# Chunk inverses four products at a time in the quarters of the array, and scan steps ranked ahead of the fill

## The chip, the core and the metric

The kernel runs on one core of a Trainium2 chip. The metric is device time in microseconds (us) of one execution. The engines are named as the profile names them: PE is TensorE (PEld its weight loads), DVE is VectorE, ACT is ScalarE, POOL is GpSimd, SP issues transfers.

## What is computed

Two blocks run one after the other on a sequence of 256 latent tokens and 256 context tokens, width 1024, all float32. The first has a feed-forward part, a mixer and a second feed-forward part. The second has two layers; its first layer mixes by RWKV-7 heads beside latent attention (MLA), each layer ends in a mixture of experts. Modulation vectors come from matrices `w_ada` and `ada_w`.

The change lies in the RWKV scan of the second block. Eight heads of width 64, two directions, states from the context carried to the latents:

```python
def step(S, inp):
    r_t, w_t, k_t, v_t, a_t, b_t = inp
    sa = jnp.einsum('bhij,bhj->bhi', S, a_t)
    S = (S * w_t[:, :, None, :] + sa[..., None] * b_t[:, :, None, :]
         + v_t[..., None] * k_t[:, :, None, :])
    return S, jnp.einsum('bhij,bhj->bhi', S, r_t)
...
y_c, states_c = rwkv_scans(r_c, v_c, dirs_c, (zero, zero))
y_l, _ = rwkv_scans(r_l, v_l, dirs_l, states_c)
```

## The kernel before

**The scan in chunks.** The kernel does not step through tokens. It cuts 256 tokens into 4 chunks of 64 and needs, for each head, direction and chunk, the inverse of a 64x64 unit triangular matrix. `rwkv` handles one half of the heads (four) at a time; two head pairs x 4 chunks give x = 0 to 7, and each pair holds one head in partitions 0 to 63 and the other in 64 to 127 (`par`). So one tile of 128 x 512 holds sixteen 64x64 matrices. The scan runs for two halves on the context and two on the latents: four inverses.

**The inverse.** A first set of products builds the matrices from `AR` and `BK` (masked by `copy_predicated` into a tile that ScalarE had filled with identities); then six levels double the block that is inverted. A level takes `Gt` times `tm` into PSUM tile `pg` (from `sm()`) and `tm` times `Gt` into `pgt` (from `acc()`); VectorE multiplies both by masks `lv` into new tiles `ab_T` and `ab_Gt`. The last level has the second product alone, copied by ScalarE. The product of each head stays in its own half of the partitions: operands and result in rows 0 to 63, or in rows 64 to 127, that is in the two quadrants on the array's diagonal. The two directions (`d`) alternate. Every float32 product of this kind shows as two records (passes) in the trace, and as one instruction in the orders below. One inverse has 416 products: 32 for each of 6 sets and 16 in the last, for two directions.

**What lies beside it.** `mixer_ab` interleaves generators by a string: `0` and `1` are the two halves of the scan, `L` the latent attention, `O` the output projection, `T` one step of `tick()`, the fill. On the context the fill is the first block's feed-forward part and its modulation; on the latents it is the modulation of the second layer. The framework's scheduler then orders the instructions of each engine by rank (the place in the program) and by its own timeline of what is ready.

**Weights.** `w()` loads 512 KB into one of four buffers `w_raw` over SP's queue; ScalarE rounds it to `w_hi`, VectorE (POOL for some) forms `w_lo`; two buffers each. A product by weights is three matmuls: `h_h,w_hi`, `h_l,w_hi`, `h_h,w_lo` (L238 to L240). The modulation multiplies `w_raw` directly in 128x32 column tiles (`sm<-w_raw,aT`, L224).

**PSUM.** In the two phases concerned `acc()` and `sm()` draw on one pool: three tiles on the context and four on the latents.

Of the kernel before, what the change touches and what calls it, by code (L numbers as in the profile page):

```python
# [14 lines left out]
U32 = mybir.dt.uint32  # L15
AF = mybir.ActivationFunctionType
OP = mybir.AluOpType
# [115 lines left out]
class _Net:  # L133
# [926 lines left out]
    def col(self, n, j):  # L1060
        c = self.pcn[n] + j
        return self.pc[:, c:c + 1]
# [36 lines left out]
    def mixer_ab(self, ht, keep, is_x, result):  # L1099

        nc, io = self.nc, self.io
        w_in = io["ab_w_in_2"][0]
        pool = nc.gpsimd
        col = self.col


        def mixed(blocks, dst):
            def use(pair, ps):
                n = len(pair)
                pp, s = self.t(2, 258, name="ab_pp"), self.t(2, 256, name="ab_s")  # L1110
                pool.memset(pp[:, :, 0:258:257], 0.0)
                self.act(pp[:, :n, 1:257], ps[:, :n, :])
                self.tt(s[:, :n], pp[:, :n, 0:256], pp[:, :n, 2:258], OP.add, e=pool)
                for a, (c0, _) in enumerate(pair):
                    b = c0 // 128
                    o = dst(b)
                    self.act(o, ps[:, a, :], scale=col(("rw_mu_2", -1.0), b))
                    self.stt(o, s[:, a], col(("rw_mu_2", 0.5), b), o, OP.mult, OP.add)
            return self.proj_T(ht, w_in, 8, [(128 * b, 128) for b in blocks], use)
        LO = [self.t(256, name="ab_lo") for _ in range(3)]  # L1120
        for _ in mixed((12, 13, 14), lambda b: LO[b - 12]):
            pass
        self.tick()

        w2, a2 = [self.t(512, name="ab_lw") for _ in range(2)]
        self.dma(w2, io["rw_w2_2"][0].rearrange("d r f -> (d r) f"))
        self.dma(a2, io["rw_a2_2"][0].rearrange("d r f -> (d r) f"))
        self.act(LO[0], LO[0], AF.Tanh)
        self.act(LO[2], LO[2], AF.Sigmoid)
        sg = {}  # L1130
        for d in range(2):
            r = slice(64 * d, 64 * d + 64)
            b0 = self.row("rw_w0_2", d * 512, 512)
            for i in range(2):
                pz = self.acc()
                self.mm(pz, LO[0][r, i * 128:(i + 1) * 128], w2[r, :])
                sg[d, i] = self.t(512, name="ab_sg")
                self.tt(sg[d, i], pz, b0, OP.add)
                self.act(sg[d, i], sg[d, i], AF.Sigmoid)
        outs = {}  # L1140
        r0, r1 = [self.rwkv(hf, mixed, LO, sg, a2, keep, is_x, outs) for hf in range(2)]
        la = self.within(self.stream("la0" if is_x else "lac", s=8, h=2, sm=2), self.mla(ht, keep, is_x, outs))
        w_out = io["ab_w_out_2"][0]

        def leave():

            todo, use = {"la": (4, 512), 0: (2, 0), 1: (2, 256)}, None
            while todo:
                key = next((z for z in todo if z in done), None)
                if key is None:  # L1150
                    yield
                    continue
                nk, r = todo.pop(key)
                use = use or self.gated_to(*result())
                for c in (0, 512):
                    ps = [self.acc() for _ in range(2)]
                    for k0 in range(0, nk, 2):
                        wt = self.w(w_out[r + k0 * 128:r + k0 * 128 + 256, c:c + 512], 2, 512, nc.gpsimd if c else None)
                        for i in range(2):
                            for k in range(2):  # L1160
                                self.mm3(ps[i], outs[key].pair(k0 + k, i * 128, 128), (wt[0][:, k, :], wt[1][:, k, :]),
                                         k0 + k == 0, k0 + k == nk - 1)
                            if k0 + 2 == nk:
                                use(i, c, 512, ps[i])
                        yield
        out = self.within(self.stream("ad0", sm=2) if is_x else self.slots, leave())
        done = set()
        streams = {"0": (r0, 0), "1": (r1, 1), "L": (la, "la"), "O": (out, "O")}
        for z in ORDERS["x" if is_x else "ctx"]:
            if z == "T":  # L1170
                self.tick()
            elif z in streams:
                g, name = streams[z]
                if next(g, self) is self:
                    done.add(name)
        for g, name in (streams[z] for z in "0L1O"):
            if g is out:
                done.update((0, 1, "la"))
            for _ in g:
                self.tick()  # L1180
            done.add(name)

    def rwkv(self, hf, mixed, LO, sg, a2, keep, is_x, outs):

        nc, lv, col = self.nc, self.lv, self.col
# [6 lines left out]
        for d in range(2):  # L1192
            r = slice(64 * d, 64 * d + 64)
            ps = self.sm()
# [15 lines left out]
        ps = self.head_spread(rr)  # L1210
# [7 lines left out]
        AR, BK, Dc = [], [], []  # L1218
        ks = self.t(2, 256, name="ab_ks")
        for d in range(2):  # L1220
            E, En = self.t(2, 4, 65, name="ab_E"), self.t(2, 4, 64, name="ab_En")
            pe = self.sm()
            for b, c in enumerate(blk):
                for i in range(2):
                    o = b * 256 + i * 128
# [32 lines left out]
        self.tt(ks, ks, R, OP.mult, e=pool)  # L1258


        def v8(z):
            return z.rearrange("p (x t) -> p x t", x=8)

        def mk(d, l, kept):
            return lv[:, 12 * kept + 6 * d + l, None, :].to_broadcast([128, 8, 64])
        GG = {}
        for d in range(2):
            tm, Gt = self.t(8, 64, name="ab_T"), self.t(8, 64, name="ab_Gt")
            for which, dst in ((0, tm), (1, Gt)):
                ps = self.sm() if which else self.acc()  # L1270
                for x in range(8):
                    for par in range(2):
                        r = slice(64 * par, 64 * par + 64)
                        a, b = AR[d][r, x // 4, x % 4, 0, :], BK[d][r, x // 4, x % 4, 1 - x % 2, :]
                        if which:
                            a, b = b, a
                        self.mm(ps[r, x * 64:(x + 1) * 64], a, b)
                self.act(dst, self.id64[:, None, :].to_broadcast([128, 8, 64]))
                m = self.lm.bitcast(U32)[:, 2 * which + d, None, :].to_broadcast([128, 8, 64])
                nc.vector.copy_predicated(dst, m, v8(ps))  # L1280
            GG[d] = tm, Gt
            yield
        for l in range(1, 7):
            for d in range(2):
                tm, Gt = GG[d]
                pgt = self.acc()
                pg = self.sm() if l < 6 else None
                halves = (slice(0, 64), slice(64, 128))
                for x in range(8):
                    for r in halves if l < 6 else ():  # L1290
                        self.mm(pg[r, x * 64:(x + 1) * 64], Gt[r, x, :], tm[r, x, :])
                    for r in halves:
                        self.mm(pgt[r, x * 64:(x + 1) * 64], tm[r, x, :], Gt[r, x, :])
                tm, Gt = self.t(8, 64, name="ab_T") if l < 6 else None, self.t(8, 64, name="ab_Gt")
                if l < 6:
                    self.tt(tm, v8(pg), mk(d, l, 0), OP.mult)
                    self.tt(Gt, v8(pgt), mk(d, l, 1), OP.mult)
                else:
                    self.act(Gt, v8(pgt))
                GG[d] = tm, Gt  # L1300
                yield

        VT = self.t(2, 256, name="ab_VT")
        ps = self.sm()
# [41 lines left out]
        for step in range(4):  # L1346
            now, G1 = [ahead.pop((step, d)) for d in range(2)], []
            Zs = [keep.get(("Z", d, hf)) for d in range(2)]
            for d, (c, ru, SC, UV, ST) in enumerate(now):
                Z = Zs[d]  # L1350
                pg = self.sm()
                at = [(pg[r, b * 64:(b + 1) * 64], r.start) for h, r, b in heads]
                parts = [[(*o, SC[:, h, 0:64], UV[:, h, :]) for o, (h, r, b) in zip(at, heads)]]
# [30 lines left out]
            for d, (c, ru, SC, UV, ST) in enumerate(now):  # L1384
                tok = slice(64 * c, 64 * c + 64)
                py = self.sm()
                at = [(py[r, b * 64:(b + 1) * 64], r.start) for h, r, b in heads]
                parts = [[(*o, UV[:, h, :], SC[:, h, 64:128]) for o, (h, r, b) in zip(at, heads)]]
# [15 lines left out]
        ps = self.sm()  # L1404
# [5 lines left out]
        ps = self.sm()  # L1410
# [743 lines left out]
```

## Time and profile before

| | us |
|---|---|
| median of 3 runs | 2460.53 (2452.52 to 2464.1) |
| the profiled execution | 2464.48 |
| its span (first to last instruction) | 2462.6 |
| TensorE busy | 2201.6 |
| VectorE busy | 1462.5 |
| ScalarE busy | 1149.5 |

The four inverses lie at 225 to 386 us and 565 to 699 us (context, first and second half of the heads), and at 1484 to 1560 us and 1621 to 1704 us (latents). A stretch of the trace is described by the busy time of each engine in it, the granted clock of TensorE (1.00 is 2.4 GHz, 0.50 is 1.2 GHz) and what the transfer engines moved.

### The profile page before, as it was taken

What the parts mean: (1) busy time and instruction counts of PE and PEld (TensorE: products, weight loads), DVE (VectorE), ACT (ScalarE), POOL (GpSimd) and SP (SyncE); (2) the same over time, 40 slices, a digit from 0 to 9 for tenths busy, and PEclk for the clock granted to TensorE, in tenths of its full rate; (3) what the DMA queues carried; (4) which work ended last, traced back from release to release, by engine and by line L of the source; (5) the groups of instructions that cost most, each with busy time, mean ns of one, the idle gap of its engine ahead of it and who ended that gap; (6) DMA issues with size and microseconds to landing.
All of it is one profiled execution on the core that took longest, in us unless ns stands there. A gap on an engine that the chain in (4) does not pass through costs nothing. (4 is left out here: it accounts for less than half of the span.)

```text
span 2462.6 us, 42928 instructions
## 1 busy us (share of the span) xinstructions
PE 2201.6 (89%) x17189; PEld 1768.4 (72%) x17189; DVE 1462.5 (59%) x2405; ACT 1149.5 (47%) x1787; POOL 482.1 (20%) x402
## 2 busy tenths in 40 slices
PE   5898999989999889988899889989899987788996
PEld 2686667878888668877799778667676666457774
DVE  2444343576555745887655544554666677756776
ACT  1453223465455434554444453434347754555673
POOL 1232000042000320000100133242215533001442
PEclk9899999999999899999999999979899998898998
DMA  8766777554444433431766556720249983224996
GB/s 289 236 199 214 251 243 257 183 163 126 129 124 135 142 125 103 137 98 40 235 190 185 162 163 203 253 77 19 95 157 342 385 308 123 52 72 142 307 326 239
DMA packets 371881, 445.07 MB, mean 181 GB/s; under 512 B 21224, under 2 KB 274264, under 8 KB 371672
## 3 DMA queue, kind: packets, MB, share of 16 engines
q1 hardware_dynamic: 362744, 409.99, 52.3%
q0 software_dynamic: 4320, 15.47, 2.0%
q10 hardware_dynamic: 4608, 16.78, 1.7%
q8 instruction: 137, 2.24, 0.4%
q14 instruction: 72, 0.59, 0.1%
HBM read 415.99 MB, written 26.96 MB: 180 GB/s over the span
## 5 line engine op out<-in xcount | busy, mean ns | idle before, releaser
L246 ACT ACTIVATE w_hi<-w_raw 128x1024 fp32r<-128x1024 f32 (+2 forms) x550 | 575.3, 1050 | 785.1 <-PE acc L240 298.2
L252 DVE TENSOR_TENSOR w_lo<-w_raw,w_hi 128x1024 fp32r<-128x1024 f32 (+1 forms) x466 | 586.8, 1265 | 460.6 <-ACT w_hi L246 455.1
L238 PE MATMUL acc<-h_h,w_hi 128*128 128x256 f32 (+1 forms) x1392 | 400.3, 288 | 16.4 <-ACT w_hi L246 11.5
L240 PE MATMUL acc<-h_h,w_lo 128*128 128x256 f32 (+1 forms) x1392 | 401.0, 288 | 4.2 <-DVE w_lo L252 3.2
L239 PE MATMUL acc<-h_l,w_hi 128*128 128x256 f32 (+1 forms) x1392 | 392.9, 282 | 1.0 <-DVE h_l L252 0.6
L238 PEld LDWEIGHTS acc<-h_h,w_hi 128*128 128x128 f32 (+1 forms) x1392 | 264.1, 190 | 29.1 <-ACT w_hi L246 15.5
L240 PEld LDWEIGHTS acc<-h_h,w_lo 128*128 128x128 f32 (+1 forms) x1392 | 263.7, 189 | 18.2 <-DVE w_lo L252 6.2
L252 POOL TENSOR_TENSOR w_lo<-w_raw,w_hi 128x1024 fp32r<-128x1024 f32 (+1 forms) x84 | 202.4, 2424 | 345.1 <-ACT w_hi L246 336.4
L239 PEld LDWEIGHTS acc<-h_l,w_hi 128*128 128x128 f32 (+1 forms) x1392 | 264.1, 190 | 2.5 <-DVE h_l L252 1.3
L224 PE MATMUL sm<-w_raw,aT 128*32 128x256 f32 x1344 | 113.9, 413 | 23.8 <-DMA w_raw<-in_w_ada 11.0
L239 PE MATMUL acc<-w_lo,h_h 128*128 128x512 f32 (+1 forms) x304 | 119.0, 392 | 0.8 <-DVE w_lo L252 0.8
L238 PE MATMUL acc<-w_hi,h_h 128*128 128x512 f32 (+1 forms) x304 | 112.7, 396 | 5.4 <-ACT h_h L246 3.8
L240 PE MATMUL acc<-w_hi,h_l 128*128 128x512 f32 (+1 forms) x304 | 116.9, 387 | 0.1
L239 PE MATMUL acc<-w_lo,mo_e_h 128*128 128x512 f32 x256 | 105.3, 411 | 12.1 <-DVE w_lo L252 11.4
L252 POOL TENSOR_TENSOR rs_r<-rs_t,mhalf 128x1 f32<-128x1 f32 (+2 forms) x37 | 39.5, 1069 | 354.1 <-DVE rs_t L256 352.8
L238 PE MATMUL acc<-w_hi,f_a_h 128*128 128x512 f32 x264 | 103.4, 415 | 4.8 <-ACT w_hi L246 2.9
L238 PE MATMUL acc<-w_hi,mo_e_h 128*128 128x512 f32 x256 | 104.0, 406 | 2.9 <-ACT w_hi L246 2.8
L239 PE MATMUL acc<-w_lo,f_a_h 128*128 128x512 f32 x264 | 105.9, 408 | 0.0
L224 PE MATMUL acc<-ab_Gt,ab_T 64*64 64x64 f32 x1536 | 103.7, 228 | 0.0
L240 PE MATMUL acc<-w_hi,f_a_l 128*128 128x512 f32 x264 | 102.5, 401 | 0.0
L240 PE MATMUL acc<-w_hi,mo_e_l 128*128 128x512 f32 x256 | 101.7, 397 | 0.0
L224 PEld LDWEIGHTS acc<-ab_Gt,ab_T 64*64 64x64 f32 x1536 | 82.7, 139 | 25.1 <-issue 21.5
(530 smaller groups left out, 4381.8 us busy)
## 6 DMA issues: line engine op xcount, KB each, us to landing
w_raw<-in_ffn_w_in SPq DMA_DIRECT2D x132, 512.0 KB
w_raw<-in_ada_w SPq DMA_DIRECT2D x96, 512.0 KB
w_raw<-in_w_ada SPq DMA_DIRECT2D x72, 512.0 KB
w_raw<-in_ffn_w_out SPq DMA_DIRECT2D x66, 512.0 KB
w_raw<-in_moe_w_gate SPq DMA_DIRECT2D x128, 256.0 KB
w_raw<-in_moe_w_up SPq DMA_DIRECT2D x128, 256.0 KB
w_raw<-in_moe_w_down SPq DMA_DIRECT2D x64, 512.0 KB
w_raw<-in_mix_w_in SPq DMA_DIRECT2D x42, 512.0 KB
```

Of the source, the lines that this page charges most:

```text
L224: self.nc.tensor.matmul(out, lhsT=lhsT, rhs=rhs, start=start, stop=stop, **kw)
L238: mm(out, lhsT=l[0], rhs=r[0], start=start, stop=False)
L239: mm(out, lhsT=l[0], rhs=r[1], start=False, stop=False)
L240: mm(out, lhsT=l[1], rhs=r[0], start=False, stop=stop)
L246: self.nc.scalar.activation(out, in_, f, **kw)
L252: (e or self.nc.vector).tensor_tensor(out=out, in0=a, in1=b, op=op)
```

## The change

First, each step of the two scan streams runs inside `high_priority(offset=5000)`: its instructions get a rank 5000 places ahead of where they stand, so the scheduler prefers them to fill, attention and output projection whenever they are ready.

Second, in the inverse the eight x are parted by `q = x % 2`. Both factors of one q lie in one tile `ab_T` (2 x 4 x 64), and so do both products in one PSUM tile (`acc()` for q = 0, `sm()` for q = 1). `quarters` issues the products so that four neighbours have the row halves and column halves (0,0), (1,1), (0,1), (1,0): for q = 1 the result lands in the other half of the partitions, and comes back a level later. The last level stays a loop of its own, on the diagonal. The number of products and the number and size of the element-wise instructions stay as they were.

```diff
--- before.py
+++ after.py
@@ -1171,7 +1171,10 @@
                 self.tick()
             elif z in streams:
                 g, name = streams[z]
-                if next(g, self) is self:
+
+                with self.tc.high_priority(offset=5000) if z in "01" else contextlib.nullcontext():
+                    ended = next(g, self) is self
+                if ended:
                     done.add(name)
         for g, name in (streams[z] for z in "0L1O"):
             if g is out:
@@ -1258,47 +1261,62 @@
         self.tt(ks, ks, R, OP.mult, e=pool)
 
 
-        def v8(z):
-            return z.rearrange("p (x t) -> p x t", x=8)
-
-        def mk(d, l, kept):
-            return lv[:, 12 * kept + 6 * d + l, None, :].to_broadcast([128, 8, 64])
+
+
+        def mk(d, l):
+            return lv[:, 6 * d + l:24:12, None, :].to_broadcast([128, 2, 4, 64])
+
+        def quarters(parts, at, l):
+            for j in range(4):
+                for which in range(2):
+                    for q in range(2):
+                        for par in range(2):
+                            r, o = [64 * (par ^ (q & (z % 2))) for z in (l, l + 1)]
+                            self.mm(parts[q][o:o + 64, (which * 4 + j) * 64:(which * 4 + j + 1) * 64], *at(q, j, which, slice(r, r + 64)))
+
+        def v4(z):
+            return z.rearrange("p (w j t) -> p w j t", w=2, j=4)
         GG = {}
         for d in range(2):
-            tm, Gt = self.t(8, 64, name="ab_T"), self.t(8, 64, name="ab_Gt")
-            for which, dst in ((0, tm), (1, Gt)):
-                ps = self.sm() if which else self.acc()
-                for x in range(8):
-                    for par in range(2):
-                        r = slice(64 * par, 64 * par + 64)
-                        a, b = AR[d][r, x // 4, x % 4, 0, :], BK[d][r, x // 4, x % 4, 1 - x % 2, :]
-                        if which:
-                            a, b = b, a
-                        self.mm(ps[r, x * 64:(x + 1) * 64], a, b)
-                self.act(dst, self.id64[:, None, :].to_broadcast([128, 8, 64]))
-                m = self.lm.bitcast(U32)[:, 2 * which + d, None, :].to_broadcast([128, 8, 64])
-                nc.vector.copy_predicated(dst, m, v8(ps))
-            GG[d] = tm, Gt
+            ps = [self.acc(), self.sm()]
+
+            def factors(q, j, which, r):
+                x = 2 * j + q
+                a, b = AR[d][r, x // 4, x % 4, 0, :], BK[d][r, x // 4, x % 4, 1 - q, :]
+                return (b, a) if which else (a, b)
+            quarters(ps, factors, 0)
+            GG[d] = []
+            for q in range(2):
+                dst = self.t(2, 4, 64, name="ab_T")
+                self.act(dst.rearrange("p w j t -> p (w j) t"), self.id64[:, None, :].to_broadcast([128, 8, 64]))
+                m = self.lm.bitcast(U32)[:, d:4:2, None, :].to_broadcast([128, 2, 4, 64])
+                nc.vector.copy_predicated(dst, m, v4(ps[q]))
+                GG[d].append(dst)
             yield
-        for l in range(1, 7):
+        for l in range(1, 6):
             for d in range(2):
-                tm, Gt = GG[d]
-                pgt = self.acc()
-                pg = self.sm() if l < 6 else None
-                halves = (slice(0, 64), slice(64, 128))
-                for x in range(8):
-                    for r in halves if l < 6 else ():
-                        self.mm(pg[r, x * 64:(x + 1) * 64], Gt[r, x, :], tm[r, x, :])
-                    for r in halves:
-                        self.mm(pgt[r, x * 64:(x + 1) * 64], tm[r, x, :], Gt[r, x, :])
-                tm, Gt = self.t(8, 64, name="ab_T") if l < 6 else None, self.t(8, 64, name="ab_Gt")
-                if l < 6:
-                    self.tt(tm, v8(pg), mk(d, l, 0), OP.mult)
-                    self.tt(Gt, v8(pgt), mk(d, l, 1), OP.mult)
-                else:
-                    self.act(Gt, v8(pgt))
-                GG[d] = tm, Gt
+                ps = [self.acc(), self.sm()]
+
+                def factors(q, j, which, r):
+                    tm, Gt = [GG[d][q][r, z, j, :] for z in range(2)]
+                    return (tm, Gt) if which else (Gt, tm)
+                quarters(ps, factors, l)
+                got = []
+                for q in range(2):
+                    got.append(self.t(2, 4, 64, name="ab_T"))
+                    self.tt(got[q], v4(ps[q]), mk(d, l), OP.mult)
+                GG[d] = got
                 yield
+        for d in range(2):
+            ps = self.acc()
+            for x in range(8):
+                for r in (slice(0, 64), slice(64, 128)):
+                    tm, Gt = [GG[d][x % 2][r, z, x // 2, :] for z in range(2)]
+                    self.mm(ps[r, x * 64:(x + 1) * 64], tm, Gt)
+            Gt = self.t(8, 64, name="ab_Gt")
+            self.act(Gt, ps.rearrange("p (x t) -> p x t", x=8))
+            GG[d] = None, Gt
+            yield
 
         VT = self.t(2, 256, name="ab_VT")
         ps = self.sm()
```

**Order on PE, context, first half of the heads.** Before, products of the inverse stand among modulation (`w_raw,aT`) and feed-forward (`f_a`) products:

```order
L224 MATMUL acc<-ab_Gt,ab_T 64x64
L224 MATMUL sm<-w_raw,aT_137 32x256 x4
L224 MATMUL acc<-ab_Gt,ab_T 64x64 x3
L224 MATMUL sm<-ab_T,ab_Gt 64x64 x2
L224 MATMUL acc<-ab_Gt,ab_T 64x64
L224 MATMUL sm<-w_raw,aT_137 32x256
L238 MATMUL acc<-w_hi,f_a_h 128x512 x2
L224 MATMUL sm<-w_raw,aT_137 32x256 x3
L224 MATMUL acc<-ab_Gt,ab_T 64x64
L224 MATMUL sm<-ab_T,ab_Gt 64x64 x2
L224 MATMUL acc<-ab_Gt,ab_T 64x64 x2
```

After, at the same place of the inverse (`ab_T` names both factors; a level of one direction has 32 products):

```order
L224 MATMUL acc<-ab_T 64x64 x15
L224 MATMUL sm<-ab_T 64x64 x14
L224 MATMUL acc<-ab_T 64x64
L224 MATMUL sm<-ab_T 64x64 x2
L224 MATMUL acc<-ab_T 64x64 x15
L224 MATMUL sm<-ab_T 64x64 x14
L224 MATMUL acc<-ab_T 64x64
L224 MATMUL sm<-ab_T 64x64 x2
L224 MATMUL acc<-ab_T 64x64 x15
L224 MATMUL sm<-ab_T 64x64 x14
```

The fill has moved out: from the first to the last product of this inverse there were 71 pieces before, spread over the instructions 1087 to 2259 of PE, and 5 pieces after, in 1085 to 1552. Fill alone now fills the instructions 1930 to 2610, where it uses 72 weight tiles; from 2610 on the two orders agree. A piece of 15 in `acc` followed by 14 in `sm` holds products of one q each.

**Order on PE, latents, first half of the heads.** Before, a level stands unbroken by the fill's products:

```order
L224 MATMUL sm<-ab_T,ab_Gt 64x64 x2
L224 MATMUL acc<-ab_Gt,ab_T 64x64 x2
L224 MATMUL sm<-ab_T,ab_Gt 64x64 x2
L224 MATMUL acc<-ab_Gt,ab_T 64x64 x2
L224 MATMUL sm<-ab_T,ab_Gt 64x64 x2
L224 MATMUL acc<-ab_Gt,ab_T 64x64 x2
L224 MATMUL sm<-ab_T,ab_Gt 64x64 x2
L224 MATMUL acc<-ab_Gt,ab_T 64x64 x2
```

After, a later level has one product by weights (`h`, `w`) between every one or two of its own:

```order
L238 MATMUL acc<-h_h,w_hi 128x256
L224 MATMUL acc<-ab_T 64x64 x2
L239 MATMUL acc<-h_l,w_hi 128x256
L224 MATMUL acc<-ab_T 64x64 x2
L240 MATMUL acc<-h_h,w_lo 128x256
L224 MATMUL sm<-ab_T 64x64
L238 MATMUL acc<-h_h,w_hi 128x256
L224 MATMUL sm<-ab_T 64x64
L239 MATMUL acc<-h_l,w_hi 128x256
L224 MATMUL acc<-ab_T 64x64 x2
L240 MATMUL acc<-h_h,w_lo 128x256
L224 MATMUL acc<-ab_T 64x64 x2
```

The pieces of this inverse go from 17 to 45. Counted over the stretch of the context (instructions 1087 to 5400), PE changes between divisions of the array (128x128, 128x32, 64x64 and so on) 463 times before and 345 after; over that of the latents (8380 to 10500) 275 times before and 322 after.

## Rows read from the trace of the kernel before

**Rows 1.** The page: engine totals, granted clock by slice, two costliest groups

```profile
PE 2201.6 (89%) x17189; PEld 1768.4 (72%) x17189; DVE 1462.5 (59%) x2405; ACT 1149.5 (47%) x1787; POOL 482.1 (20%) x402
...
PEclk9899999999999899999999999979899998898998
...
L246 ACT ACTIVATE w_hi<-w_raw 128x1024 fp32r<-128x1024 f32 (+2 forms) x550 | 575.3, 1050 | 785.1 <-PE acc L240 298.2
...
L252 DVE TENSOR_TENSOR w_lo<-w_raw,w_hi 128x1024 fp32r<-128x1024 f32 (+1 forms) x466 | 586.8, 1265 | 460.6 <-ACT w_hi L246 455.1
```

**Rows 2.** Table of stretches; the first row names the columns

```profile
core 0: us, PE busy (x) PEld busy (x) DVE busy (x) ACT busy (x) POOL busy (x), PEclk, DMA share, GB/s
10.00:80.00 70.00, 48.97 (x380) 25.48 (x380) 13.71 (x41) 13.05 (x22) 5.29 (x8) 0.88 0.89 308
80.00:217.00 137.00, 125.23 (x990) 105.18 (x992) 64.07 (x93) 64.85 (x101) 43.12 (x36) 0.98 0.72 213
217.00:446.00 229.00, 213.39 (x2293) 157.82 (x2292) 92.72 (x133) 66.39 (x92) 8.38 (x11) 0.98 0.74 242
565.00:699.00 134.00, 131.01 (x1452) 111.48 (x1450) 78.47 (x107) 57.33 (x80) 11.29 (x12) 0.99 0.42 127
1484.00:1560.00 76.00, 73.36 (x1233) 61.94 (x1233) 32.87 (x61) 20.89 (x36) 18.16 (x17) 1.00 0.66 212
1621.00:1704.00 83.00, 75.16 (x1032) 57.59 (x1033) 46.00 (x93) 27.73 (x66) 29.70 (x37) 0.84 0.10 30
```

**Rows 3.** Waits, 217 to 446 us: waiter, releaser, us in total, times, longest

```profile
ACT w_hi L246 <- DMA w_raw<-in_ffn_w_in: 76.8, 19, 8.1
...
ACT w_hi L246 <- DMA w_raw<-in_ffn_w_out: 30.4, 8, 6.8
...
SPq L221 <- PE sm L224: 48.9, 28, 4.8
...
SPq L221 <- DVE w_lo L252: 39.8, 22, 6.7
```

**Rows 4.** Timeline of TensorE, 1640.5 us: start, length, instruction

```profile
1640.61 0.28 PE L224 MATMUL acc<-ab_Gt,ab_T 64*64 64x64 f32 x4
1640.73 0.28 PE L224 MATMUL sm<-ab_T,ab_Gt 64*64 64x64 f32 x4
1640.85 0.28 PE L224 MATMUL acc<-ab_Gt,ab_T 64*64 64x64 f32 x4
1640.96 0.28 PE L224 MATMUL sm<-ab_T,ab_Gt 64*64 64x64 f32 x4
```

**Rows 5.** Timeline of TensorE, 258.9 us

```profile
258.98 0.28 PE L239 MATMUL acc<-h_l,w_hi 128*128 128x256 f32 x1
259.09 0.28 PE L240 MATMUL acc<-h_h,w_lo 128*128 128x256 f32 x1
259.30 0.27 PE L224 MATMUL acc<-ab_Gt,ab_T 64*64 64x64 f32 x1
259.31 0.27 PE L224 MATMUL sm<-ab_T,ab_Gt 64*64 64x64 f32 x1
```

**Rows 6.** Timeline of TensorE, 250 to 270 us, column tiles

```profile
254.19 0.64 PE L224 MATMUL sm<-w_raw,aT 128*32 128x256 f32 x8
...
259.79 1.07 PE L224 MATMUL sm<-w_raw,aT 128*32 128x256 f32 x16
```

**Rows 7.** Timeline of TensorE, 1824.5 us

```profile
1824.59 0.73 PE L224 MATMUL sm<-tokr,mo_hot 128*128 128x1 bf16 x23
```

**Rows 8.** Instructions by tile, ab_T then ab_Gt: ns least, median, most; idle before

```profile
L252 DVE TENSOR_TENSOR ab_T<-sm,lv x40: 680/684/692, 251.5 to 1700.0; 128x512 f32<-128x512 f32 x40
...
L1280 DVE COPY_PREDICATED ab_T<-lm,acc x8: 717/728/756, 230.6 to 1630.5; 128x512 f32<-128x512 uint32 x8
...
its engine sat idle before it (us, times) until:
...
  DVE ab_Gt L252: 4.8, 5
...
  DVE ab_T L252: 0.8, 2
...
L252 DVE TENSOR_TENSOR ab_Gt<-acc,lv x40: 680/682/692, 255.4 to 1700.6; 128x512 f32<-128x512 f32 x40
...
L1280 DVE COPY_PREDICATED ab_Gt<-lm,sm x8: 714/727/741, 231.5 to 1631.6; 128x512 f32<-128x512 uint32 x8
```

**Rows 9.** Table of stretches, where the clock was lower

```profile
228.00:235.00 7.00, 5.99 (x34) 5.76 (x36) 4.30 (x6) 1.98 (x3) 2.59 (x3) 0.52 0.48 155
1672.00:1679.00 7.00, 7.00 (x70) 5.20 (x71) 2.12 (x7) 1.38 (x3) 0.37 (x1) 0.51 0.01 2
```


## The prediction

> **What bounds the kernel now.** I read the totals first. TensorE is busy for 2201.6 of 2462.6 us, VectorE for 59% and ScalarE for 47% [rows 1]; the clock slices show the high level of 2.4 GHz nearly everywhere. So time goes where TensorE waits, or where its own work is cut, and I ask next which stretches have which limit. The table of stretches [rows 2] covers the four inverses. Context, first half (217 to 446 us): TensorE busy 213.4 of 229.0 us at 242 GB/s, so 15.6 us are left over and the weight transfers are close behind. Context, second half (565 to 699): 131.0 of 134.0, TensorE is the limit and transfers are light (127 GB/s). Latents, first half: 73.4 of 76.0. Latents, second half: 75.2 of 83.0 at a mean granted clock of 0.84, with hardly any transfer.
>
> The waits of 217 to 446 us say why TensorE stands there [rows 3]: ScalarE's split of a weight tile waited 76.8 + 30.4 us for weights, while the transfer queue itself waited 48.9 us for TensorE and 39.8 us for VectorE to free a buffer. The two limits alternate: four raw tiles of 512 KB are all that transfers can run ahead.
>
> Last I read what a product costs. In the even stretch of the second half each group of four records (two 64x64 products of two passes) starts 0.12 us after the one before [rows 4]; two records at a time start 10 ns apart or less (259.30 and 259.31) [rows 5]. Two diagonal quadrants therefore work at once, a pass holds its quadrant for 58 ns, and a record costs 29 ns. Coming from another shape of tile costs more: 259.09 to 259.30 is 0.21 us, where the same products follow each other after 0.12 [rows 5]. That is 0.09 us for a change of the array's division.
>
> **The change part by part.**
>
> *Products in four quarters.* The count stays: 4 inverses x 416 = 1664 products, 3328 records. In pairs that is 3328 x 29 ns = 96.5 us; counted along the order of before, where some stand without a partner, 101.0 us. After, 384 of each 416 are issued so that four neighbours lie in four quadrants (the last level stays on the diagonal). Do four run at once? No row has four 64x64 tiles; the nearest are the 128x32 tiles, where 16 records take 1.07 us and 8 take 0.64 [rows 6], 54 ns for each more, though one such record moves 256 columns and a full-array record of 256 columns takes 0.12 us by itself [rows 5]. So four divisions of the array do overlap. Bounds: nothing (0 us), or the whole half (11.1 us per inverse, 44 in all). But fours are kept only where both PSUM tiles are free: the new order has long pieces of 15 products into acc and then 14 into sm, which are pairs again. Counted along the order at 58 ns a pass and quadrant I get 18.8, 18.0, 20.1 and 18.2 us against 26.1, 25.2, 24.6 and 25.2: **-7.3, -7.2, -4.5 and -7.0, together -26 us**.
>
> At this place a rule of the Trainium skill speaks against the change: "TensorE: Matmul & The Clock Gate", section "Wait — 56ns, not 53.3ns?", says that matmuls never start closer than about 25 ns. By that rule four records would cost 100 ns, not 58. The smallest products here obey it: 23 records of 128x1 take 0.73 us [rows 7], 25 to 26 ns each after the first. The pairs do not, since different quadrants start within 10 ns [rows 5]. I go by these; the other is a rival below.
>
> *Changes of division.* Along the order they fall in the context from 463 to 345 (63 of the 118 in the first half, where the inverse now comes in 5 pieces instead of 71) and rise in the latents from 275 to 322, where single products now alternate with single products by weights. At 0.09 us: **-10.7 and +4.3 us**. Bounds: 0, where TensorE waits anyway, and the full amount.
>
> *The lump without fill.* Element-wise work is the same in number and size: VectorE takes 684 and 682 ns for each multiplication and 728 and 727 for a masked copy [rows 8]. A level of both directions needs 4 x 0.684 = 2.7 us of VectorE, against as much of TensorE (18.8 over 7 levels). Before, fill lay beside this, and TensorE waited only 4.8 + 0.8 us in four inverses for VectorE's factors [rows 8]; now it has nothing else. With two directions alternating I take +3 us in the first half and +2 in the second, each bounded by 0 and by the 16.6 us of VectorE's work laid end to end (20 x 0.684 + 4 x 0.728).
>
> *The fill that comes after.* This is the part with the widest bounds. In the context's first half, the stretch from the inverse's start to the point from which both orders agree holds the same fill; after the change nearly none of it lies in the inverse, the last 680 products are fill alone and eat 72 tiles (37.7 MB) in 100 us of TensorE time. That needs 377 GB/s. No stretch in the context got it: 217 to 446 ran at 242, the best long stretch, 10 to 80 us, at 308 [rows 2]. At 308 those tiles take 122 us, less 7 for four tiles held ready: 115. TensorE's need in the whole stretch is 213.4 - 7.3 - 5.7 + 3 = 203, of which 103 lie ahead. So 103 + 115 = 218 against 229: **-11 us**. Bounds: transfers that keep up, 203 (-26); transfers at 242 GB/s, 103 + 149 = 252 (+23). I take 308, because here, as at 10 to 80 us, nothing but weights is wanted, and at 308 a tile comes every 1.7 us, while ScalarE takes 1.05 and VectorE 1.27 us to split one [rows 1].
>
> *Queues.* The weights' order on SP stays. POOL and ScalarE get the scan's steps earlier; they are less than half busy [rows 1], so I set nothing for them. VectorE's split of weights queues behind the scan's multiplications; its price is in the +3.
>
> *Sum,* against the profiled execution (2464.48 us, span 2462.6): context first half -11 (its -7.3, -5.7 and +3 are inside); second half -7.2 - 5.0 + 2 = -10; latents -11.5 + 4.3 = -7. Together -28: 2436.5. The median of the runs shown, 2460.53, is 4 us below the profiled one: **2433 us**.
>
> **Rivals.**
>
> *1. Quarters pay little.* Records cost 25 ns whatever the quadrant (the skill's rule above would be its reason). Half of the records run in fours: 1664 x 4 ns = -7, against -26. Then the second half has -1.7 - 5 + 2 = -5, the latents -3.4 + 4.3 = +1, the first half 109 + 115 = 224, -5. For it: nothing in this trace runs four of them. Against it: [rows 5, 6]. Together -9: 2451.5, no change that could be told.
>
> *2. The weights become the limit: slower.* After a lump in which four buffers are full and transfers stand, 72 tiles must come at once. 80 to 217 us, also feed-forward weights, got only 213 GB/s [rows 2]; at that rate the pure fill takes 177 - 7 = 170 us, the stretch 103 + 170 = 273, +44, and with -10 and -7 the sum is +27: 2487. It decides from 233 GB/s on downwards (162 us for the tiles, 155 after the four held ready, +29 in the stretch, +12 in all). TensorE waiting for weights speaks for more: where it was busy for only 5.99 of 7 us the granted clock was 0.52, the level of 1.2 GHz, and it fell to 0.51 once in the midst of steady work (1672 to 1679) [rows 9]. Against it: in 217 to 446 the queue waited for buffers 48.9 + 39.8 us, so 242 is not what the transfers could do.
>
> *3. The fill keeps up and the fours hold.* First half -26, second half -13 (no stall), latents -12: -51, that is 2409. For it: 308 GB/s was held beside a start in which TensorE was itself busy 49.0 of 70 us, so not the ceiling either.
>
> *4. The ranks change the latents for the worse.* There the new order breaks fours up by one product by weights each, and attention pieces now wait for whole levels. With nothing saved in the latents and +5 for the clock in a second half that has 0.84 already: -21 + 5 = -16: 2444.5.
>
> **How the numbers follow.** A measurement of this kernel tells about 0.5% (12.3 us) from no change. The forecast has 0.46 (2418 to 2447), rival 1 0.18, rival 2 0.14, rival 3 0.13, rival 4 0.09. Faster by over 0.5% means under 2448: all of the forecast and of rival 3, most of rival 4, together 0.66. Within 0.5%: rival 1 and the rest of 4, 0.20. Slower: 0.14. The range of 8 in 10 starts below rival 3's value, at 2405, and leaves out the upper part of rival 2: to 2464. The forecast's own range is 2418 to 2447.
>
> **What will show it.** The records ab_T in the new profile: four within 58 ns, that is groups of eight every 0.12 us, would confirm the quarters; 25 ns between neighbours rival 1. In the context the stretch from about 217 us to the end of its fill should be 218 us long, with little transfer in the first 20 and over 300 GB/s in the last 115; 230 or less there is rival 2. Waits of "DVE ab_T for PE" should shrink and "PE for DVE ab_T" appear, some microseconds in each half. The second half of the context should be about 124 us instead of 134, and its second lump at the high clock; a clock of 0.5 in the lumps makes the prediction wrong, since two lumps of 18 us at half speed cost more than the quarters bring.

## The result, and the profile after

The changed kernel takes 2506.2 us (median of 4 runs, 2504.64 to 2510.01) against 2461.07: a ratio of 1.0169, 95% interval 1.0141 to 1.0198. It is slower, where 2433 us was forecast. Its profiled execution took 2510.01 us with a span of 2508.1, 45.5 us more than before.

First the totals of the page after, which answer to [rows 1]: busy time of each engine.

```profile
PE 2196.7 (88%) x17189; PEld 1760.7 (70%) x17189; DVE 1467.3 (59%) x2405; ACT 1144.8 (46%) x1782; POOL 481.5 (19%) x402
```

TensorE has 5 us less to do and stands idle 50 us longer. Where, is seen by cutting both traces at the same TensorE products (numbered in the order of PE, at numbers where the orders agree). The cells are the time between their starts, in us, in one profiled execution of each kernel; the ratio is of medians of several executions.

| kernel | context, 1st half (1087-2996) | context, 2nd half and exit (2996-5400) | latents (8380-10500) | ratio to before |
|---|---|---|---|---|
| before | 284.5 | 387.6 | 320.7 | 1 |
| changed | 300.5 | 389.7 | 340.2 | 1.0169 |
| ranks alone | 306.2 | 394.8 | 365.9 | 1.0332 |
| quarters alone | 286.0 | 380.0 | 310.3 | 0.994 |
| quarters, ranks on the context | 307.0 | 389.8 | 314.8 | 1.0066 |
| quarters, ranks on the latents | 284.9 | 382.9 | 342.9 | 1.0086 |
| changed, 6 raw buffers | 275.3 | 389.4 | 345.3 | 1.0032 |
| quarters, 6 raw buffers | 273.6 | 385.5 | 307.4 | 0.9867 |
| before, 6 raw buffers | 273.0 | 380.5 | 322.4 | 0.991 |
| quarters, latents' 1st half ranked | 289.6 | 379.3 | 319.2 | 0.9996 |
| quarters, latents' 2nd half ranked | 280.4 | 379.4 | 317.8 | 0.9983 |
| quarters, latents ranked unequally | 288.3 | 381.3 | 321.7 | 0.9978 |
| quarters, 6 raw, context's 2nd half ranked | 272.2 | 384.4 | 308.3 | 0.9881 |
| quarters, 6 raw in both | 272.3 | 381.8 | 302.7 | 0.9827 |

How far a cell can be trusted: five of these kernels have the same context stage (quarters, no ranks, four buffers), and its first cell lies between 280.4 and 289.6. Less than 9 us there says nothing. The other two columns repeat within 4 us and 8 us where the code is the same (for the latents: 310.3, 307.4, 314.8 and 308.3). A profiled execution need not be a typical one either: that of the changed kernel with six buffers (2486.3 us) is the slowest of its ten, 13 us above their median, and those with one half of the heads ranked on the latents (2459.21 and 2451.89) are the fastest of theirs, 7 and 8 us below. Where the total of a kernel matters, the ratio decides.

Of the changed kernel's 45.5 us, 16.0 lie in the first cell, 2.1 in the second, 19.5 in the third, and 7.9 in the stretches not shown.

**The context.** The table of stretches after, where [rows 2] had one row of 217 to 446 us with TensorE busy 213.4 of 229 (columns as there):

```profile
226.00:256.00 30.00, 25.36 (x794) 22.99 (x794) 20.70 (x30) 4.85 (x7) 4.38 (x5) 0.94 0.30 101
256.00:330.00 74.00, 69.37 (x629) 49.21 (x624) 26.47 (x45) 23.53 (x45) 1.23 (x4) 0.98 0.63 207
330.00:460.00 130.00, 102.44 (x801) 72.64 (x800) 42.66 (x55) 31.70 (x38) 1.65 (x1) 0.97 0.80 259
```

And, in one row, as many products as the 229 us before held:

```profile
219.70:458.50 238.80, 201.05 (x2298) 148.29 (x2297) 91.48 (x132) 63.99 (x97) 9.19 (x12) 0.97 0.68 222
```

The lump of the inverse (226 to 256) is short and moves 101 GB/s; the fill alone (330 to 460) moves 259 GB/s, and TensorE stands 27.6 us in it. It waits for weights that have not been split, and these for their transfer, in the waits of 330 to 460 us (waiter, releaser, us, times, longest):

```profile
ACT w_hi L246 <- DMA w_raw<-in_ffn_w_in: 58.8, 13, 7.2
PEld acc L238 <- ACT w_hi L246: 28.2, 20, 3.0
PE acc L238 <- ACT w_hi L246: 19.6, 16, 2.6
```

The transfer queue meanwhile waits for a buffer. It is not the split that holds the buffers (DVE `w_lo`, 1.0 us) but TensorE, which has yet to read the modulation tiles in them (PE `sm`):

```profile
SPq L221 <- PE sm L224: 48.1, 28, 4.0
SPq L221 <- DVE w_lo L252: 1.0, 2, 0.7
```

**The latents.** Rows for the middle of the first inverse there (products 8800 to 9200), before and after:

```profile
1519.60:1560.10 40.50, 40.00 (x669) 34.07 (x669) 17.06 (x29) 11.83 (x20) 8.17 (x8) 1.00 0.71 224
```

```profile
1544.60:1602.70 58.10, 54.91 (x658) 42.33 (x658) 17.08 (x30) 12.63 (x20) 8.15 (x8) 0.84 0.55 176
```

Hardly fewer records (658 for 669), 18 us more, TensorE "busy" for 15 of them at a mean granted clock of 0.84. (The orders do not agree at these two numbers, so the stretches hold slightly different work.) Its timeline shows why: first at the high clock, then a few us later at the low one.

```profile
1566.11 0.38 PE L238 MATMUL acc<-h_h,w_hi 128*128 128x256 f32 x1
1566.42 0.32 PE L224 MATMUL acc<-ab_T 64*64 64x64 f32 x2
1566.68 0.39 PE L239 MATMUL acc<-h_l,w_hi 128*128 128x256 f32 x1
1566.99 0.33 PE L224 MATMUL sm<-ab_T 64*64 64x64 f32 x2
1567.25 0.38 PE L240 MATMUL acc<-h_h,w_lo 128*128 128x256 f32 x1
...
1571.00 0.58 PE L240 MATMUL acc<-h_h,w_lo 128*128 128x256 f32 x1
1571.51 0.47 PE L224 MATMUL acc<-ab_T 64*64 64x64 f32 x2
1571.91 0.58 PE L238 MATMUL acc<-h_h,w_hi 128*128 128x256 f32 x1
```

One product of the inverse and one by weights take 0.57 us a turn (1566.11 to 1566.68) and 0.91 at the low clock (1571.00 to 1571.91). Unbroken they cost 0.12 for the product by weights [rows 5] and 0.06 for the other [rows 4]: 0.18. A turn at the high clock is 0.39 us dearer. The clock, in stretches:

```profile
1563.00:1570.00 7.00, 7.00 (x60) 4.91 (x58) 0.88 (x2) 2.27 (x4) 3.41 (x3) 1.00 0.53 166
1570.00:1580.00 10.00, 10.00 (x39) 7.54 (x39) 0.00 (x0) 0.00 (x0) 0.00 (x0) 0.51 0.02 6
```

After 7 us in which TensorE alternated and started only 60 records, 1.2 GHz was granted for 10 us. The same came once before in this inverse: from 1532 us on the two kinds of product alternate, and from 1536 to 1546 the clock is 0.50.

**The quarters.** In a piece that stays whole, the timeline of TensorE in the context's first inverse reads:

```profile
249.04 0.22 PE L224 MATMUL sm<-ab_T 64*64 64x64 f32 x1
249.04 0.22 PE L224 MATMUL acc<-ab_T 64*64 64x64 f32 x1
249.05 0.22 PE L224 MATMUL sm<-ab_T 64*64 64x64 f32 x1
249.05 0.22 PE L224 MATMUL acc<-ab_T 64*64 64x64 f32 x1
249.10 0.22 PE L224 MATMUL sm<-ab_T 64*64 64x64 f32 x1
```

Four records start within 0.01 us and the next four 0.06 us later: four quadrants work at once, at 58 ns a pass, twice the rate of [rows 4].

### The profile page after: what moved, and what is told of

It is laid out like the page before. It is cut to its first block, busy times and chain, and to the rows that moved or that the text cites. A ratio compares the mean times of both kernels' runs of the same rounds, so it can differ in the third digit from the quotient of the medians.

```text
span 2508.1 us, 42953 instructions
## 1 busy us (share of the span) xinstructions
PE 2196.7 (88%) x17189; PEld 1760.7 (70%) x17189; DVE 1467.3 (59%) x2405; ACT 1144.8 (46%) x1782; POOL 481.5 (19%) x402
## 5 line engine op out<-in xcount | busy, mean ns | idle before, releaser
L239 PE MATMUL acc<-h_l,w_hi 128*128 128x256 f32 (+1 forms) x1392 | 399.4, 287 | 0.2 <-DVE h_l L252 0.2
L239 PE MATMUL acc<-w_lo,mo_e_h 128*128 128x512 f32 x256 | 105.3, 411 | 12.1 <-DVE w_lo L252 11.5
L252 POOL TENSOR_TENSOR x<-x,gate 128x512 f32<-128x512 f32 x12 | 18.4, 1548 | 424.2 <-ACT junk L246 330.7
L224 PE MATMUL sm<-diag,x 128*128 128x128 f32 x256 | 50.5, 356 | 46.4 <-DVE diag L256 40.6
```

What stands on the lines that cost most here:

```text
L224: self.nc.tensor.matmul(out, lhsT=lhsT, rhs=rhs, start=start, stop=stop, **kw)
L239: mm(out, lhsT=l[0], rhs=r[1], start=False, stop=False)
L252: (e or self.nc.vector).tensor_tensor(out=out, in0=a, in1=b, op=op)
```

## The experiments

**Which half of the change costs the time?** Theory A: the order; theory B: the quarters. Four kernels, each with one part.

*Ranks alone* (before, with the first hunk of the change). 

> The kernel before with the ranks alone (inverse in pairs, as it was). Theory A, the order costs the time: the inverse is pulled ahead of the fill as in the changed kernel and has 21 us more of products, so 2500 to 2530 us, the context's first half again slower from its inverse to the common point, with over 40 us of the fill's TensorE time waiting for weights. Theory B, the quarters cost the time (results that cross the halves, tiles that come free one q at a time): 2465 us or less.

Measured 2543.51 us, 1.0332 (1.0279 to 1.0384): slower still, as A said, and above the upper end that it gave. The quarters make up about half of that loss again, most of it on the latents (340.2 us for 365.9).

*Quarters alone.*

```diff
-                with self.tc.high_priority(offset=5000) if z in "01" else contextlib.nullcontext():
-                    ended = next(g, self) is self
-                if ended:
+                if next(g, self) is self:
                     done.add(name)
```

> The changed kernel without the ranks: quarters alone, fill spread through the inverse as before. Theory A: the inverse's products take about 77 us instead of 98 and nothing else moves much, so 2435 to 2450 us. Theory B: 2480 us or more.

Measured 2450.42 us, 0.994 (0.9915 to 0.9964), 0.4 us over A's upper end. Theory B falls. Against the changed kernel (1.0169) the ranks cost 2.3%.

*Ranks on the context alone* (`if z in "01" and not is_x else`) and *on the latents alone* (`and is_x`).

> The changed kernel with the ranks on the context alone. Theory A: the context keeps its +18 to +24 us, the latents lose their +22, so 2475 to 2490 us. Theory B: unchanged, about 2505 us.

> The changed kernel with the ranks on the latents alone. Theory A: the latents keep their +22 us or some of it and the context gains by the quarters (about -10), so 2465 to 2480 us. Theory B: unchanged, about 2505 us.

Measured 2480.97 us, 1.0066 (1.0038 to 1.0094), and 2488.2 us, 1.0086 (1.0057 to 1.0114), the second above the 2465 to 2480 expected. By the table the ranks cost 21.0 and 9.8 us in the two context stages (14.5 and 9.7 by the changed kernel, which has the same code there), and 32.6 us on the latents (29.9).

**Why does the context lose?** Theory C: four raw buffers hold the transfers down, since a tile occupies its buffer from issue until it has been used. Theory D: the transfers themselves. Two more buffers, in the context's stage alone:

```diff
-                    with self.phase("ab1", f=8, b=18, q=8, sm=3):
+                    with self.phase("ab1", f=8, b=18, q=7, sm=3), self.pool("wxc", reuse_waits="tile") as self.wx:
+                        self.more = dict(raw=2, hi=0)
...
-        p, n = self.w_pool("raw", 3)
+        p, n = self.w_pool("raw", self.more["raw"])
```

(the same for `hi`; elsewhere `more` keeps 3 and 1.)

> The changed kernel with six raw weight buffers instead of four, in the context's RWKV stretch alone (one work buffer of 256 columns less there). Theory C, the fill that is left alone runs at 250 to 270 GB/s because only four tiles can be under way between issue and split: with six the rate rises above 300 GB/s, TensorE waits less, and the kernel comes to 2480 to 2492 us. Theory D, the transfers themselves give no more than that: within 5 us of the changed kernel's 2506.

Measured 2473.65 us, 1.0032 (1.0012 to 1.0052), better than C asked. In its trace the stretch of the same fill, and then its waits, read:

```profile
330.00:440.00 110.00, 98.57 (x758) 72.72 (x758) 42.17 (x56) 30.97 (x37) 1.65 (x1) 0.94 0.89 298
```

```profile
PEld acc L239 <- ACT w_hi L247: 9.8, 7, 2.2
SPq L222 <- PE sm L225: 27.3, 22, 4.1
```

298 GB/s for 259, just short of the 300 expected; the weight loads of a tile's first products wait 9.8 us instead of 28.2, and the queue 27.3 us for modulation tiles instead of 48.1. D falls as it was put. But half as many buffers again gave 1.15 times the rate, so the buffers are not the only limit: the transfer engines' share rose from 0.80 to 0.89, the share that 10 to 80 us had at 308 GB/s [rows 2]. The first context stage is 275.3 us, as good as without ranks (273.6): what the ranks cost there with four buffers, 14 to 21 us, is gone with six.

> Quarters without ranks, and the same six raw buffers on the context. Theory C: the first half there, which gained nothing by the quarters (waits for weights took it), gives back up to 10 us: 2436 to 2446 against 2450 for quarters alone. Theory D: 2447 to 2453.

Measured 2433.04 us, 0.9867 (0.983 to 0.9904), just better than C's range.

> The kernel before (pairs, no ranks) with the six raw buffers on the context: what the quarters are worth where weights do not bind. The inverse in quarters without ranks took 69 us of TensorE instead of 98, but gave 14 us. Theory G, the rest was lost to waits for weights in the context's first half: then six buffers with pairs come to 2455 to 2462 us, 22 to 29 above quarters with six buffers (2433). Theory H, the rest is lost elsewhere: 2445 to 2450.

Measured 2446.92 us, 0.991 (0.9874 to 0.9945): H. The buffers are worth 11 to 12 us in the first stage with pairs as with quarters (284.5 to 273.0, 286.0 to 273.6), and the quarters nothing visible there with either number. With six buffers quarters and pairs are 14 us apart (2433.04 and 2446.92), and the table puts all of it on the latents (307.4 for 322.4). What the shorter inverse sets free on the context is not on the path there; which wait takes it was not settled.

**Why do the latents lose?** Theory E: the pieces (17 in the first inverse with no ranks, 66 with). Theory F: ranked steps hold other work back.

> Quarters, and ranks for the first half of the heads on the latents alone. The first inverse there comes in 37 pieces, against 17 with no ranks and 66 with ranks for both halves, whose projections then compete with it at equal rank. Theory E, the pieces cost the time (each entry and exit changes the array's division, and the clock falls in such a stretch): +24 us for 49 pieces more is 0.5 us each, so +10 for 20 more: about 2460. Theory F, the ranks cost by holding attention and projections back: with stream 1 unranked about 2475 or more.

> Quarters, and ranks on the latents alone, with 5000 for the first half of the heads and 2500 for the second, so that the second half's projections no longer compete at equal rank. The first inverse comes in 37 pieces instead of 66, the second in 15; divisions change 240 times in the stretch. Theory E (the pieces cost): 12 us less than with equal ranks (2488), so 2470 to 2478. Theory F (held-back attention costs): no better than 2485.

The edits are `if z == "0" and is_x else`, and `offset=5000 if z == "0" else 2500` on the latents. Measured 2466.06 us, 0.9996 (0.9982 to 1.001), and 2462.93 us, 0.9978 (0.9955 to 1.0001): the first 6 us above what E said, the second 7 below.

Neither time can be read by the number of pieces in these expectations. Most of the breaks that make 37 come from products `ab_AR,ab_BK`, which are 64x64 themselves, so the array keeps its division. Counted in the traces with such breaks left out, the first inverse comes in 15 pieces in both kernels, against 17 with no ranks and 44 with equal ranks (the 45 of the order above); the divisions change 271 and 262 times over the latents' column, against 279 and 344. So E, by division, gives these two kernels no loss at all, and yet they are 0.4 to 0.6% slower than quarters alone. The rows of that column tell the two losses apart. Quarters alone, unequal ranks, equal ranks (the latents alone ranked):

```profile
1471.20:1782.00 310.80, 272.63 (x3695) 205.94 (x3695) 179.67 (x394) 126.12 (x269) 91.05 (x97) 0.91 0.43 139
```

```profile
1471.30:1793.40 322.10, 275.14 (x3695) 213.36 (x3694) 179.85 (x393) 126.33 (x269) 91.56 (x97) 0.91 0.41 134
```

```profile
1470.40:1813.00 342.60, 302.05 (x3696) 228.84 (x3695) 183.49 (x392) 126.97 (x268) 91.31 (x96) 0.89 0.39 126
```

With equal ranks TensorE is busy 29.4 us longer over the same number of records and stands about as long as with none (40.6 and 38.2 us): that is E, and unequal ranks undo nearly all of it (2.5 us). With unequal ranks it is TensorE's idle time that grows, by 8.8 us: that is F. In the medians the step from equal to unequal ranks is worth 1.1% (1.0086 to 0.9978), and 0.4% remain over quarters alone (0.994). At equal rank the second half's projections, which are products by weights, come in between the first half's inverse.

How much of E is the turn and how much the clock can be estimated from the middle of the inverse (products 8800 to 9200), which takes 58.1 us in the changed kernel and this with quarters alone:

```profile
1515.00:1554.30 39.30, 36.04 (x668) 29.38 (x668) 17.02 (x29) 11.34 (x19) 8.17 (x8) 1.00 0.74 232
```

There are 29 pieces in it for 10, and 18 of the 29 are lone products: at 0.39 us each about 7 us. A mean clock of 0.84 for 1.00 over 58.1 us is about 9 us. The two make most of the 18.8 us. No run held the clock apart from the turns.

> Quarters, and ranks for the second half of the heads on the latents alone. The inverses come in 17 and 14 pieces and the array changes its division 261 times in the stretch, against 276 with no ranks. Theory E: no pieces more, so no loss: 2440 to 2452. Theory F: attention is held back behind the second half's steps: 2460 or more.

Measured 2459.72 us, 0.9983 (0.9965 to 1.0001): above what E gave, at the edge of what F gave, with no piece more. So F has a part here too. It can be looked for in the second inverse (products 9548 to 10130). Rows of quarters alone, second half ranked, both halves ranked, and first half alone ranked:

```profile
1612.90:1692.30 79.40, 66.46 (x1038) 49.30 (x1037) 50.44 (x101) 33.80 (x77) 31.89 (x39) 0.85 0.10 31
```

```profile
1604.70:1689.30 84.60, 67.58 (x1049) 51.87 (x1050) 50.12 (x102) 32.75 (x75) 32.94 (x39) 0.83 0.09 30
```

```profile
1635.00:1723.40 88.40, 68.54 (x1050) 53.39 (x1051) 51.40 (x102) 32.79 (x75) 33.14 (x39) 0.84 0.09 28
```

```profile
1611.10:1701.60 90.50, 73.47 (x1050) 52.80 (x1048) 49.49 (x101) 33.10 (x76) 31.95 (x39) 0.77 0.09 28
```

In the first three TensorE has nearly the same work, 66.5 to 68.5 us, but stands 12.9, 17.0 and 19.9 us. Transfers are light. The attention lies here beside the scan, and TensorE's waits for the attention's own steps (tiles `at_`, `mla_`) are 3.4 us with no ranks, 7.9 with the second half ranked and 10.3 with both. Two of the last:

```profile
PE at_pp L243 <- DVE at_mx L256: 3.0, 2, 1.6
PE at_s L224 <- ACT at_pt L246: 2.1, 3, 0.7
```

That fits attention and scan no longer covering each other's gaps, but it is read from waits; no run took the attention away. And the fourth row warns: where this half is not ranked and only the first is, the stretch is no shorter. TensorE stands 17.0 us there as well, with only 4.8 for the attention, and the clock is at 0.77. What the ranks of the first half cost here stays open.

**Does anything beat both?** Two kernels with six buffers: ranks for the context's second half (`if z == "1" and not is_x`), and six buffers on the latents as well (the same pool in the phase `ab0`).

> Quarters, six raw buffers, and ranks for the second half of the heads on the context alone (46 and 13 pieces, 382 changes of division in the context against 439). If only weights and pieces matter: 5 us less than quarters with six buffers, 2425 to 2431. If spending the fill early leaves the end of the context's stretch without cover, as in the changed kernel (10 us more there): 2438 to 2448.

> Quarters without ranks, six raw buffers on the context and on the latents. In the latents' first half quarters alone left TensorE 7 us less busy (134.4 of 146.0 us, against 141.3 of 147.0) and no faster. If it waits for weights there too, the stretch from the projections to the end of the second half is 5 to 10 us shorter and the kernel comes to 2420 to 2430 us, ratio 0.982 to 0.985. If the wait is for other work, or the lower clock takes the gain, it stays at 2430 to 2438, ratio 0.986 to 0.988.

The first: 2439.9 us, 0.9881 (0.9847 to 0.9916). The time lies in the second range, but the ratio is not to be told from 0.9867, and the context's second stage (384.4 us for 385.5) shows neither a gain nor a loss: inconclusive. The second: 2423.43 us, 0.9827 (0.9796 to 0.9858), the fastest of the study, 1.7% under the kernel before, and inside the range expected if TensorE waits for weights there too. Its latents take 302.7 us against 307.4 and 310.3; that is within what this column repeats to, and the interval of the ratio overlaps that of six buffers on the context alone.

## Why the prediction was wrong, point by point

Measured minus forecast is 73.5 us in the profiled executions (+45.5 for -28). Four steps make it up.

1. *The fill that comes after*, 27 us of it: -11 was forecast, +16.0 came (300.5 for 284.5; this cell repeats only to 9 us). The mechanism was the one described, lump and then starving fill; the rate was wrong. To the end of the prediction's own stretch it took 238.8 us for the 218 forecast. TensorE's need there was right (201 us busy for 203), its idle time was not: 38 us for 15. I took 308 GB/s from the stretch 10 to 80 us, because "at 308 a tile comes every 1.7 us" and the split is faster. The fill had 259. If all four buffers of 0.524 MB are always in use, that is 8.1 us a tile from issue to release, and 308 would be 6.8. The split is not what took the time (1.0 us of the queue's waits): the buffers were held by modulation tiles that TensorE had yet to read (48.1 of 130 us, where 10 to 80 us of the kernel before had 16.7 of 70), while TensorE itself waited for feed-forward weights. That wait stood in [rows 3] with 48.9 us, and rival 2 counted it against itself. In 10 to 80 us nearly all tiles were modulation tiles (only 4 were split), in 330 to 460 us 22 of 512 KB were split: the row was taken from another mixture. My bound of 242 GB/s (+23) held the truth. Rival 2 had place and direction right and, with 213 GB/s, too high a price.

2. *Changes of division on the latents*, with the inverse there: -7 was forecast, +19.5 came. The part of the quarters was right as far as this column tells: -11.5 forecast, -10.4 without ranks (310.3 for 320.7). What failed is the term of the order, 0.09 us for each of 47 changes more, +4.3; the ranks cost 29.9 us there (340.2 for 310.3). A change was priced from a row that has one change among many products of a kind. A lone product has one on either side, 0.18 us, and its turn costs 0.39: its own two passes stand behind each other with no neighbour in another quadrant, and it starts later behind a product by weights (0.31 us after it, where [rows 5] had 0.21). On top of that comes the clock, which the term left out; rival 4 had put +5 on it, for the second half of the heads. And what the second inverse gained in products (67.8 us busy for 77.5 before) went into standing: it takes 88.3 us after, 88.9 before. That part was put at nothing; it is F above, and its cause is not settled.

3. *The context's second half*, 12 us: -10 forecast, +2.1. Quarters without ranks gave -7.6 there (with six buffers nothing: 385.5 for 380.5). With ranks the inverse passes earlier, but the way out of the stage, from product 5200 to 5400, takes 81 us with ranks and 71 without. All five kernels that rank the second half on the context lose 9 to 11 us there against those that do not, with four buffers and with six. That the fill which covered this way out has been used up is the likely reason; no run shows it by itself. My sum ended with the inverse.

4. *Outside these stretches* I had nothing, and 7.9 us came, in three pieces of 2 to 3.

What held: the quarters run four at once, and rival 1 (25 ns a record) is refuted by the row at 249.04. Counted from start to start along the trace the four inverses take 19.4, 16.4, 21.1 and 19.8 us, 76.7 in all, against 97.9 before: -21 for the -26 forecast. Without ranks more fours stay whole, and it is 68.9. (Such a count depends on where a piece is taken to end; other rules give -23 to -28 for the -21.) The lumps did not fall to the low clock, by which the prediction would have been wrong at once: 0.94 in 226 to 256 us, 0.97 in 593 to 661. Their stall was small as taken: idle time of TensorE before `ab_T` that VectorE's factors ended, in the instructions by tile after, for 4.8 + 0.8 us in [rows 8]:

```profile
  DVE ab_T L252: 10.2, 8
```

So the step that failed is the price of the new order, in two terms: 308 GB/s for the fill that is left alone, where 259 came, and 0.09 us for a change of division on the latents, where a lone product costs 0.39 and the clock falls as well. Both prices were read from rows of another order. The gains were counted in full, and what the ranks take away (cover for weights, cover for a stage's end, whole pieces) was put too small or at nothing.

## What to carry to other kernels

Fill spread through a latency-bound chain also gives the weights time to arrive: pull the chain out, and the fill runs at (buffers x tile) / (time from issue to release). Take that time from a stretch with the same mixture of tiles, and do not take it to stay: with four buffers it was 8.1 us here and with six 10.6 (at 298 GB/s, if all are in use). If the chain's products are short and use another division of the array, count in the new order the pieces that change the division, and price a piece from a row that has one alone; a break by products of the same division is not such a piece. And raising the ranks of two streams at once lets them cut each other up, which unequal ranks undid; here no ranks and two more buffers (0.9827) beat every ranked order.

## What the runs showed of the hardware

- Four float32 products of 64x64 in four quadrants run together: four records every 58 ns, two of them into one PSUM tile and two into another (249.04 us).
- A lone product between two full-array products costs 0.39 us over its share (0.57 us a turn), where each change of division by itself was read as 0.09 us. In the starts behind the rows shown, the two passes of such a lone product are 106 or 107 ns apart; products in the middle of a piece follow at 58.
- The granted clock fell from 2.4 to 1.2 GHz in a stretch in which TensorE never stood but alternated single products (1.00 in 1563 to 1570 us, 0.51 in 1570 to 1580), and was at 0.91 in the 2 us after. At the low clock the turn takes 0.91 us for 0.57.
- Six raw buffers for four moved the same fill from 259 to 298 GB/s (330 to 460 and 330 to 440 us), with the transfer engines' share at 0.89 for 0.80.
